# One encoder block on one core: attention fillers dealt anew over the steps, the conv branch's weights released inside the last conv split, and three orderings of the MLP

## The chip, the cores and the metric

The kernel runs on one core of one Trainium2 chip. A core has five engines with their own instruction streams: TensorE (PE in the profile, with its weight loads as PEld), VectorE (DVE), ScalarE (ACT), GpSimd (POOL) and SyncE (SP, which here issues the DMAs). They meet only through semaphores. The metric is the device time of one execution, in microseconds; the median of several executions is given.

## The reference

One layer on an input of 1024 tokens by 1024 channels in float32, with 8 heads of 64, a token grid of 16 by 64 and an MLP of width 4096:

```python
u = rms_norm(x, norm1_g)
q, k, v, cb, cc, ch, ga, gb = split(u @ w_in)
q = rms_norm(q.reshape(B, S, 8, 64), q_norm_g)
k = rms_norm(k.reshape(B, S, 8, 64), k_norm_g)
y_a = neighbourhood_attention(q, k, v, rpb) @ w_attn_branch   # window 8 rows x 16 columns, softmax with a bias
y_b = (cb * conv3(cc * ch, conv_w)) @ w_conv_branch           # depthwise, width 3
merged = sigmoid(ga) * y_a + sigmoid(gb) * y_b
x = x + merged @ w_o
h = rms_norm(x, norm2_g) @ w_mlp_in
x = x + square(relu(h)) @ w_mlp_out
```

## The kernel before

Every float32 matrix product is computed from 16-bit parts: each operand is scaled by a power of two and split into a high and a low half (fp16), and three passes (high by high, high by low, low by high) are summed in PSUM. The high half is a ScalarE copy, the low half a VectorE `scalar_tensor_tensor` (operand times scale minus the high half). The scale needs the sum of squares over a whole weight block: ScalarE squares with a row sum, VectorE adds and casts to a column, and TensorE multiplies that column by ones, one 128x1 matmul that sums over the partitions (`all_sum`, L198 in the profile).

PSUM is handed out as 8 banks in three rings, "d" and "s" of three and "o" of two. The emission order is written out by hand, and each engine runs its own part of that order. `unit` emits the matmuls of a product (L207), then the follow-up work of the product before it (`settle`, the "post"), and then calls `step` and `tick` a given number of times. `step` advances the foreground generators, the follow-ups of finished products; `tick` advances the background ones, which prepare the next weights. A number of ticks per product thus decides where on each engine's stream the background work stands. `apart` makes a generator yield until a given amount of TensorE work has been emitted.

The attention loop runs 64 steps (4 pairs of heads, 8 blocks of 128 tokens, 2 heads), pipelined over 77 turns. In turn k it emits the scores of step k (`at_qk`, L828), the masked maximum on VectorE (`at_max`), the exponential on ScalarE (`at_exp`), the high half of the probabilities (`at_hi`, ScalarE), the low half (`at_lo`, VectorE, `P<-sz,sc,P`), their transposes by DMA from SP's queue for two steps at a time (`at_turn`, L878, PT<-P), and every fourth turn the value products (`at_pv(k - 12)`, L905). Between them stand **fillers**: matmuls of the conv projection (L924, from the generator `conv_mms`), 576 in all. `share(k)` says how many fillers turn k gets, and by that also how much background work `deal(k)` lets in, which uses the estimate that the `Meter` object makes of VectorE's and ScalarE's time. What is left after the loop is emitted at once. In turns 66 to 73 `turn_piece` adds the DMA transposes qD<-gs (L931).

`conv_split` turns a finished conv column into 16-bit halves; the branch weights cB may be scaled only when all four conv columns have their scales (`rowsB`), and `prep` of cB waits for `ch.ready`, which is set behind the loop. After the loop, the first gate (cG, two groups of 24 matmuls), the attention branch (w_wa), the conv branch (w_wb), the other gates and W_o follow.

Both MLP products use a scheme of seven block products in place of eight (`seven`). The first has 16 quads of 7 products of 12 matmuls each (`quad`). A quad's weights are made by `sums1` (GpSimd and ScalarE: sums of blocks, squares) and `prep1` (scale and split, tsum and w in the profile). A quad's posts add the products into `as` on VectorE; then `h_done` applies relu and square on ScalarE and makes four block sums (`sums`, L1278), on GpSimd for q > 1, and writes the result to DRAM. Its arguments wait1 and wait2 hold relu and sums back by so many steps. The activations come from `low(n, part)`, which issues DMA transposes u2T<-v and u2x<-v, one for several forms (L1327). The second MLP product has 28 products whose weights and activations `prep2` makes; the operand with number 16 + n serves its n-th product, in `ORDER`; operands 16 and 17 are made while quads 14 and 15 run.

In the profile of before nearly all VectorE and ScalarE instructions show the line L66, which is the `Meter`'s call; they are told apart by their tiles.

Of the kernel before, what the change touches and what calls it, by code (L numbers as in the profile page):

```python
# [70 lines left out]
def encoder_block(ctx: ExitStack, tc: tile.TileContext, x, weights, cols, gqk, rel, masks, out):  # L71
    nc = tc.nc
    G, T, SP = nc.gpsimd, nc.tensor, nc.sync
    V, A = Meter(nc.vector, 0.96, 150), Meter(nc.scalar, 1.2, 190)

    base = ctx.enter_context(tc.tile_pool(name="base", bufs=1))
    rawp = ctx.enter_context(tc.tile_pool(name="rawp", bufs=5))
# [35 lines left out]
    def tmp(n=1):  # L113
        return cols_of("tmp", n)

    def at(c, i, n=1):
        return slice(c.start + i, c.start + i + n)

    def mul(a, b, out=None):
        out = out or tmp(a.stop - a.start)  # L120
        V.tensor_tensor(sc[:, out], sc[:, a], sc[:, b], op=OP.mult)
        return out
# [13 lines left out]
    fg, bg = [], []  # L136
# [3 lines left out]
    def advance(g):  # L140
        try:
            return next(g) or True
        except StopIteration:
            return False

    def step(n=1):
        for _ in range(n):
            for g in list(fg):
                if not advance(g):
                    fg.remove(g)  # L150

    def tick(n=1):

        for _ in range(n):
            i = 0
            while i < len(bg):
                r = advance(bg[i])
                if not r:
                    bg.pop(i)
                elif r == WAIT and side[0]:  # L160
                    i += 1
                else:
                    break
# [19 lines left out]
    def built(*chs):  # L183

        forced[0] = True
        while not all(ch.split for ch in chs):
            tick()
            step()
        forced[0] = False
# [29 lines left out]
    def settle():  # L219
        while late:  # L220
            late.pop(0)()
# [134 lines left out]
    for (kind, j), pieces in plan():  # L356
        ch = chunks[kind, j] = Chunk(kind, [(nk, sum(n for _, n in cs)) for _, _, nk, cs in pieces],
                                     {"A": "wa", "B": "wb"}.get(kind, "ws"), rows.get(kind, lambda j: g1)(j),
                                     j if kind == "V" else None, 9 if kind in "VQKCGS" else 0)
        ch.first = len(loads)  # L360
        for p, (k, w) in enumerate(ch.widths):
            ch.offs.append(offset)
            if kind != "X" and (kind, j) != ("1", 0) and (kind, j, p) != ("1", 1, 1):
# [3 lines left out]
    cV, cConv, cA, cB, cO, c1, c2, c2x = ([chunks[k, j] for j in range(n)] for k, n in  # L367
                                              (("V", 2), ("C", 4), ("A", 4), ("B", 4), ("O", 2),
                                               ("1", 16), ("2", 4), ("X", 4)))
# [65 lines left out]
    def pow2_half(ss, top, s, inv, more=0):  # L435

        V.tensor_scalar(sci[:, ss], sci[:, ss], EXP, None, op0=OP.bitwise_and)
        yield
        V.tensor_scalar(sci[:, ss], sci[:, ss], 1.0, float(1 << 23), op0=OP.mult, op1=OP.add)
        yield  # L440
        V.tensor_scalar(sci[:, ss], sci[:, ss], 1, EXP, op0=OP.logical_shift_right, op1=OP.bitwise_and)
        yield
        V.tensor_scalar(sci[:, s], sci[:, ss], -1.0, float((190 + top) << 23), op0=OP.mult, op1=OP.add)
        V.tensor_scalar(sci[:, inv], sci[:, ss], 1.0, float((64 - top - more) << 23), op0=OP.mult, op1=OP.add)
        yield
# [131 lines left out]
    for p in range(11):  # L577
# [7 lines left out]
        for q in (p,) if p < 6 else (2 * p - 6, 2 * p - 5):  # L585
            c = q // 2 + 3
# [56 lines left out]
    for n, (kind, b) in enumerate(todo):  # L643
        ch = cQ if kind == "q" else cK
# [103 lines left out]
    def conv_split(j, cv):  # L748
        ch = cConv[j]
        m, s, inv = tmp(), tmp(), tmp()  # L750
        A.activation(BT[:, 1, j].bitcast(BF16), cv, AF.Square, accum_out=sc[:, m])
        yield
        V.tensor_scalar(sc[:, m], sc[:, m], 1e-36, None, op0=OP.max)
        yield
        yield from pow2_half(m, 14, s, inv)
        mul(inv, ch.inv, at(rowsB, j))
        G.tensor_scalar(cv, cv, sc[:, s], 1.0, op0=OP.mult, op1=OP.mult)
        yield
        bh, bl = (BT[:, w, j].rearrange("p (b r c) -> p b r c", b=8, r=16) for w in range(2))
        A.activation(bh, perm(cv), AF.Copy)  # L760
        yield
        pv = perm(cv)
        for b in range(0, 8, 2):
            G.tensor_tensor(bl[:, b:b + 2], pv[:, b:b + 2], bh[:, b:b + 2], op=OP.subtract)
# [175 lines left out]
    def scale_of(am, more, n=3):  # L940

        a, mark = am
        yield from apart(mark, n * 6144, work)
        b, s, inv = cols_of("prep", 1), cols_of("prep", 1), keep()
        yield from all_sum(a, b, anybank(), 1e-36)
        yield from pow2_half(b, 14, s, inv, more)
        return s, inv
# [30 lines left out]
        yield  # L978
        ch.s, ch.inv = yield from scale_of(am, 9, 1)

    meters, debt, mark = (V, A), [0.0, 0.0], [V.ns, A.ns]

    def share(k):
        return 9 if k < 55 else 5 if k < 67 else 2

    def account(k):
        room = 216.0 * share(k) + 570.0
# [13 lines left out]
    for k in range(N + 13):  # L1001
        p, w = k // 16, k % 16
# [37 lines left out]
    emit(1000)  # L1040
    while conv_live or conv_tail or conv_q:
        conv_step(1)
    for ch in cB:
        ch.ready = True
    built(cG)
    p2.close()
    pbias.close()

# [144 lines left out]
    for n in range(8):  # L1193
# [23 lines left out]
        else:  # L1217
# [50 lines left out]
    U2 = (u2T,  # L1268
          w4p.tile([128, 3, 2, 4, 512], F16, name="u2x", bufs=1))
# [53 lines left out]
    def low(n, part):  # L1323

        for a, b, v in pieces(n, part):
            V.tensor_tensor(v[:, :, 1], fv[0][:, a:b], v[:, :, 0], op=OP.subtract)
            SP.dma_start_transpose(U2[a // 4][:, a % 4:a % 4 + b - a, :, :, 128 * n:128 * n + 128]  # L1327
                                   .rearrange("p f s k t -> p (f s k) t"), v.rearrange("p f s k -> p (f s k)"))
        pair_done[0] = n + part

    def form_sums():
# [4 lines left out]
    pe_done, ready = [-2], set()  # L1336
# [32 lines left out]
    def prep1(q):  # L1369

        ch = c1[q]
        s, ch.inv = yield from scale_of(ch.sum, 9, 1)
        yield from gate(q)
        pool, tag = TAGS[q % 3]
        P = P1[q] = pool.tile([128, 7 if q else 8, 2, 512], F16, name="w16_1", tag=tag)
        yield from forms_split(ch, tsum[q], s, P)
        ready.add(q)
        if 1 < q < 15:
            yield from sums1(q + 1)
# [171 lines left out]
    def h_done(q, c0=0, c1=512, wait1=0, wait2=0):  # L1551

        f = AS[q] if c1 < 512 else AS.pop(q)
        v = f[:, :, c0:c1]
        yield from wait(wait1)
        A.activation(v[:, 0:4], v[:, 0:4], AF.Relu)
        yield
        A.activation(v[:, 0:4], v[:, 0:4], AF.Square, scale=sc[:, c1w[q].inv],
                     accum_out=sc[:, at(bsum[q // 4], 4 if c1 < 512 else q % 4)])
        yield  # L1560
        yield from wait(wait2)
        if q > 1:
            yield from sums(v, G)
        else:
            for _ in sums(v, V):
                pass
        if c1 < 512:
            return
        SP.dma_start(HS[q // 4][:, :, q % 4], f)
        live.remove(q)  # L1570
        if q % 4 == 3:
            m = tmp()
            V.tensor_reduce(sc[:, m], sc[:, bsum[q // 4]], axis=AX, op=OP.max)
            yield
            yield from pow2(m, 14, *R[q // 4])
            r_ready[q // 4] = True

    def quad(q, c0=0, c1=512):
        need(q)
        if c0 == 0:  # L1580
            while q - 2 in live:
                step()
            live.add(q)
            AS[q] = w4p.tile([128, 7, 512], F32, name="as", tag="as")
        ps = {}
        z = [AS[q][:, i, c0:c1] for i in range(7)]
        if q == 2:
            z[4:6] = extra

        def post6(ps):  # L1590
            V.tensor_tensor(z[5], ps[6], z[4], op=OP.add)
            if c0:
                post5(ps)

        def post5(ps):
            V.tensor_tensor(z[1], ps[5], z[5], op=OP.subtract)

        def post7(ps):
            V.tensor_tensor(z[6], ps[7], z[5], op=OP.add)
            V.tensor_tensor(z[2], ps[4], z[6], op=OP.add)  # L1600
            V.tensor_tensor(z[3], ps[5], z[6], op=OP.subtract)

        def post3(ps):
            V.tensor_tensor(z[1], ps[3], z[1], op=OP.add)
            if q == 0:
                fg.append(h_done(q, c0, c1, 3, 4 if c0 else 24))
            elif c1 == 512:
                fg.append(h_done(q, 0, c1, *((2, 6) if q == 1 else ())))
        seven(P1[q], actU2, c0, c1, {
            1: lambda ps: A.activation(z[4], ps[1], AF.Copy),  # L1610
            6: post6, 5: None if c0 else post5,
            2: lambda ps: V.tensor_tensor(z[0], ps[2], z[4], op=OP.add),
            7: post7, 3: post3}, 2 if c1 == 512 else 3, 5, (1, 2, 5, 4, 6, 7, 3) if c0 else (1, 6, 5, 4, 2, 7, 3))

    def whole(q):
        quad(q)
# [128 lines left out]
    for n in (2, 3, 4):  # L1745
        h_load(n)
    settle()
    while live:
        step()
    p4.close()  # L1750
# [29 lines left out]
    for n in range(28):  # L1780
        s, o = n // 7, n % 7
# [92 lines left out]
```

## Time and profile before

| | us |
|---|---|
| median of 3 runs | 1238.45 (1238.36 to 1238.69) |
| own time of the profiled execution | 1236.77 |
| its span | 1235.0 |
| TensorE busy | 1196.9 |
| VectorE busy | 936.9 |
| ScalarE busy | 765.9 |
| GpSimd busy | 430.3 |

All instruction times are read on the span, from its start. A timeline row has the start, the length, the engine and line, the operation with its output and inputs, the shapes and the number of instructions drawn together; brackets at the end give the idle time of the engine ahead of it and what ended it. A row of waits has the engine and the line that waited, what it waited for, the total in microseconds, the number of waits and the longest. A row of windows has its stretch, its length, the busy time and the number of instructions of PE, PEld, DVE, ACT and POOL, the granted TensorE clock as a share of the full one, the share of the DMA engines and GB/s. The mean granted clock of the span was 0.994.

### The profile page before, as it was taken

Reading aid. Unit: us, or ns where it says so; the run is one execution under the profiler, and the core shown is the slowest. Engines: PE = TensorE matmul, PEld = TensorE weight load, DVE = VectorE, ACT = ScalarE, POOL = GpSimd, SP = SyncE. Lnnn points to the kernel's source line nnn. Section 1 sums busy time; section 2 is a strip of 40 time slices with the busy share of each in tenths; the row PEclk is TensorE's granted clock in tenths of the full one; section 3 lists DMA queues with packets and bytes.
Section 4 is the critical chain, followed back from the end, with each engine's and each line's share of the span. In section 5 each row is a group of like instructions: output and inputs, shape, how many; then the busy total and the mean of one; then the engine's idle time right before and its main releaser. Section 6 shows DMA issues by size and latency. Waiting matters only on the chain.

```text
span 1235.0 us, 16691 instructions
## 1 busy us (share of the span) xinstructions
PE 1196.9 (97%) x6102; PEld 576.9 (47%) x6102; DVE 936.9 (76%) x1747; ACT 765.9 (62%) x1185; POOL 430.3 (35%) x289
## 2 busy tenths in 40 slices
PE   5989999999899999999999999999999999999998
PEld 3534445555444444444458444444444444444444
DVE  6668778888558786877878664555547999999997
ACT  6777667768644454535768777777775763646430
POOL 2440003232212111101003466655648373463562
PEclk8999999999899999999999999999999999999999
DMA  6558455565761211216096653454474844435202
GB/s 258 107 200 178 103 118 112 116 153 105 131 154 34 69 52 51 69 35 255 18 174 152 205 170 137 162 187 142 140 290 162 313 155 159 168 116 222 103 35 103
DMA packets 170867, 173.34 MB, mean 140 GB/s; under 512 B 131488, under 2 KB 132000, under 8 KB 166688
## 3 DMA queue, kind: packets, MB, share of 16 engines
q1 hardware_dynamic: 170784, 172.27, 47.2%
q8 instruction: 48, 0.79, 0.3%
q14 instruction: 35, 0.29, 0.1%
HBM read 102.51 MB, written 37.75 MB: 114 GB/s over the span
## 4 chain that ended last, share of the span: by engine, by line
PE 40%; DVE 6%; ACT 2%; issue 2%; DMA 1%; DVEq 0%; ACTq 0%
PE ps_d L207 16%; PE ps_s L207 14%; PE ps_o L207 10%; DVE as L66 1%; DVE ops L66 1%; DVE w L66 1%; DVE form L66 1%; ACT as L66 1%; DVE v L66 1%; DMA u2T<-v 1%; DMA u2x<-v 1%; ACT ops L66 1%; DVE x L66 0%; DVE sc L66 0%; ACT u2x L66 0%
## 5 line engine op out<-in xcount | busy, mean ns | idle before, releaser
L207 PEld LDWEIGHTS <-ops 128*128 128x128 f16 x1356 | 132.4, 98 | 159.9 <-issue 2.7
L207 PEld LDWEIGHTS <-w 128*128 128x128 f16 x1368 | 132.8, 98 | 143.5 <-issue 3.8
L924 PE MATMUL ps_d<-uT,w_ws 128*128 128x512 f16 x576 | 136.7, 382 | 0.0
L207 PE MATMUL ps_s<-ops 128*128 128x512 f16 (+1 forms) x528 | 118.3, 374 | 0.0
L207 PE MATMUL ps_d<-ops 128*128 128x512 f16 x504 | 115.6, 379 | 0.0
L66 ACT ACTIVATE ops<-hf,sc 128x2048 f16<-128x2048 f32 x26 | 52.0, 1999 | 94.0 <-PE ps_d L207 52.7
L207 PE MATMUL ps_d<-u2T,w 128*128 128x512 f16 (+1 forms) x504 | 110.3, 371 | 0.0
L1074 POOL TENSOR_TENSOR tsum<-raw 128x512 f32<-128x512 f32 x28 | 46.6, 1677 | 148.1 <-ACT raw L66 148.1
L207 PEld LDWEIGHTS <-uT 128*128 128x128 f16 x648 | 64.9, 101 | 70.5 <-issue 5.6
L1278 POOL TENSOR_TENSOR as<-as 128x512 f32<-128x512 f32 x56 | 76.7, 1370 | 41.4 <-ACT as L66 38.1
L207 PEld LDWEIGHTS <-w_s 128*128 128x128 f16 x588 | 56.9, 98 | 68.6 <-DVE w_s L66 0.6
L924 PEld LDWEIGHTS <-w_ws 128*128 128x128 f16 x576 | 56.1, 98 | 59.7 <-issue 2.0
L207 PE MATMUL ps_s<-u2x,w 128*128 128x512 f16 (+1 forms) x348 | 78.6, 375 | 0.0
L207 PE MATMUL ps_o<-ops 128*128 128x512 f16 x324 | 74.3, 379 | 2.4 <-DVE as L66 2.4
L66 DVE SCALAR_TENSOR_TENSOR ops<-hf,sc,ops 128x2048 f16<-128x2048 f32 x26 | 71.7, 2759 | 5.7 <-ACT ops L66 5.7
L66 ACT ACTIVATE raw<-raw,sc 128x256 f32<-128x256 f32 x172 | 71.1, 494 | 6.7 <-DMA raw<-in_weights 6.7
L66 DVE TENSOR_TENSOR as<-ps_s,as 128x512 f32<-128x512 f32 (+1 forms) x38 | 23.4, 616 | 58.5 <-ACT as L66 57.9
L66 DVE TENSOR_SCALAR sc<-sc 128x1 int32<-128x1 int32 (+3 forms) x380 | 57.6, 167 | 12.9 <-ACT sq L66 4.3
L1074 POOL TENSOR_TENSOR gsum<-raw 128x512 f32<-128x512 f32 x14 | 18.5, 1340 | 136.8 <-issue 52.3
L66 ACT ACTIVATE w<-raw,sc 128x512 f16<-128x512 f32 (+1 forms) x29 | 25.4, 920 | 50.8 <-DVE sc L66 50.8
L66 ACT ACTIVATE sz<-sz,sc 128x384 f32<-128x384 f32 (+1 forms) x64 | 37.2, 581 | 26.8 <-DVE sc L66 26.6
L66 DVE SCALAR_TENSOR_TENSOR w_ws<-raw,sc,w_ws 128x512 f16<-128x512 f32 (+2 forms) x72 | 48.5, 712 | 6.7 <-ACT w_ws L66 6.7
(261 smaller groups left out, 2548.6 us busy)
## 6 DMA issues: line engine op xcount, KB each, us to landing
raw<-in_weights SPq DMA_DIRECT2D x89, 512.0 KB, 5.5
hs<-as SPq DMA_DIRECT2D x16, 1792.0 KB, 8.7
hf<-hs SPq DMA_DIRECT2D x26, 1024.0 KB, 6.7
w2x<-in_weights SPq DMA_DIRECT2D x16, 512.0 KB, 8.3
raw<-in_weights SPq DMA_DIRECT2D x16, 384.0 KB, 3.7
xt<-in_x SPq DMA_DIRECT2D x8, 512.0 KB, 9.8
gs<-s SPq DMA_DIRECT2D x4, 1024.0 KB, 6.4
x<-in_x SPq DMA_DIRECT2D x8, 512.0 KB, 10.0
```

The source lines that it names most:

```text
L66: return f(out, *a, **kw)
L207: T.matmul(ps, l, r, start=a, stop=b)
L924: T.matmul(ps, l, r, start=a, stop=b)
L1074: G.tensor_tensor(t[:, o], a, b, op=OP.add)
L1278: sub.tensor_tensor(z[o], z[a], z[b], op=op)
```

## The change

- The filler table `share` is another: 9 a turn for the first six turns, then 8 up to turn 54, then 6, 7 and 4, in place of 9 up to turn 54, 5 and 2. The limit of `deal` and `account` follows it.
- `V` and `A` are the plain engines, and the `Meter` exists only for the attention loop.
- cB is set ready inside `conv_split(3, ...)`, when `rowsB` is complete.
- For the last pair of token blocks (n == 3) `low` issues one DMA transpose for each form, in place of one for four and one for three.
- In `prep1` the ones matmul of quads 3 to 7 stands two products behind the sum, in place of one.
- `h_done`: quad 14's block sums run on VectorE; quads 2 to 5 hold relu back by three steps, quad 14 holds the sums back by two.
- Quad 15 has three ticks a product in place of five, and behind it the program ticks until operand 17 has been emitted before it steps the live quads to their end.

```diff
-    V, A = Meter(nc.vector, 0.96, 150), Meter(nc.scalar, 1.2, 190)
+    V, A = nc.vector, nc.scalar
...
         yield from pow2_half(m, 14, s, inv)
         mul(inv, ch.inv, at(rowsB, j))
+        if j == 3:
+            for c in cB:
+                c.ready = True
...
-    meters, debt, mark = (V, A), [0.0, 0.0], [V.ns, A.ns]
+    meters = V, A = Meter(nc.vector, 0.96, 150), Meter(nc.scalar, 1.2, 190)
+    debt, mark = [0.0, 0.0], [0.0, 0.0]
 
     def share(k):
-        return 9 if k < 55 else 5 if k < 67 else 2
+        return 9 if k < 6 else 8 if k < 55 else 6 if k < 64 else 7 if k < 73 else 4
...
-    for ch in cB:
-        ch.ready = True
     built(cG)
+    V, A = nc.vector, nc.scalar
...
             V.tensor_tensor(v[:, :, 1], fv[0][:, a:b], v[:, :, 0], op=OP.subtract)
-            SP.dma_start_transpose(U2[a // 4][:, a % 4:a % 4 + b - a, :, :, 128 * n:128 * n + 128]
-                                   .rearrange("p f s k t -> p (f s k) t"), v.rearrange("p f s k -> p (f s k)"))
+            for c, d in [(f, f + 1) for f in range(a, b)] if n == 3 else [(a, b)]:
+                SP.dma_start_transpose(U2[c // 4][:, c % 4:c % 4 + d - c, :, :, 128 * n:128 * n + 128]
+                                       .rearrange("p f s k t -> p (f s k) t"),
+                                       v[:, c - a:d - a].rearrange("p f s k -> p (f s k)"))
...
-        s, ch.inv = yield from scale_of(ch.sum, 9, 1)
+        s, ch.inv = yield from scale_of(ch.sum, 9, 2 if 2 < q < 8 else 1)
...
-        if q > 1:
+        if q > 1 and q != 14:
             yield from sums(v, G)
...
-                fg.append(h_done(q, 0, c1, *((2, 6) if q == 1 else ())))
+                fg.append(h_done(q, 0, c1, *((2, 6) if q == 1 else (3, 0) if q < 6 else (0, 2) if q == 14 else ())))
...
-            7: post7, 3: post3}, 2 if c1 == 512 else 3, 5, (1, 2, 5, 4, 6, 7, 3) if c0 else (1, 6, 5, 4, 2, 7, 3))
+            7: post7, 3: post3}, 2 if c1 == 512 else 3, 5 if q < 15 else 3, (1, 2, 5, 4, 6, 7, 3) if c0 else (1, 6, 5, 4, 2, 7, 3))
...
     settle()
+    while 17 not in ready:
+        tick()
     while live:
         step()
```

## The prediction

> **What bounds the kernel now.** I read first the page's head, busy times and chain, then TensorE's waits, then the timelines at the places where it waits.
>
> ```profile
> span 1235.0 us, 16691 instructions
> PE 1196.9 (97%) x6102; PEld 576.9 (47%) x6102; DVE 936.9 (76%) x1747; ACT 765.9 (62%) x1185; POOL 430.3 (35%) x289
> PE 40%; DVE 6%; ACT 2%; issue 2%; DMA 1%; DVEq 0%; ACTq 0%
> ...
> PE ps_o L905 <- DMA PT<-P: 5.8, 3, 3.0
> PE ps_o L207 <- DVE as L66: 4.8, 2, 2.4
> PE ps_d L207 <- ACT w_wb L66: 1.5, 1, 1.5
> PE ps_s L198 <- DVE ones L66: 0.8, 1, 0.8
> PE ps_s L207 <- DMA u2T<-v: 0.2, 1, 0.2
> ```
>
> TensorE is busy 97% of the span and no matmul is taken away, so all there is to win lies in its waits (total, count, longest) and in stretches at half clock. The change touches three regions: the end of the attention loop (5.8), the conv branch weight (1.5) and the MLP's first half (0.8, 0.2, and 4.8 in two waits, one inside that half and one at the passage to the second product).
>
> The end of the attention, on TensorE (start, length, idle ahead in brackets) and by windows (length, then busy PE, PEld, DVE, ACT, POOL, granted clock, DMA share, GB/s):
>
> ```profile
> 318.53 1.18 PE L905 MATMUL ps_o<-PT,vT 128*64 128x256 f16 x24 [0.36 <-DMA PT<-P]
> 319.64 3.19 PE L924 MATMUL ps_d<-uT,w_ws 128*128 128x512 f16 x14
> 325.79 2.13 PE L905 MATMUL ps_o<-PT,vT 128*64 128x256 f16 x24 [2.96 <-DMA PT<-P]
> 327.86 2.53 PE L924 MATMUL ps_d<-uT,w_ws 128*128 128x512 f16 x8
> 332.88 1.81 PE L905 MATMUL ps_o<-PT,vT 128*64 128x256 f16 x18 [2.49 <-DMA PT<-P]
> 337.26 1.02 PE L207 MATMUL ps_o<-uT,w_ws 128*128 128x512 f16 x4
> ...
> 166.00:326.70 160.70, 157.17 (x998) 79.95 (x998) 134.24 (x401) 119.72 (x285) 36.02 (x50) 1.00 0.58 122
> 325.75:329.16 3.41, 3.37 (x28) 2.15 (x29) 0.96 (x3) 3.38 (x8) 1.73 (x3) 0.50 1.27 156
> 332.58:335.99 3.41, 3.11 (x22) 1.90 (x23) 0.63 (x1) 0.60 (x1) 1.07 (x1) 0.50 0.50 113
> ```
>
> The value products (L905) wait for probabilities, because the fillers (L924) are used up: 14, then 8, are left between the last three. Behind both long waits stands a stretch of 3.41 us at clock 0.50; it costs half of its busy time, (3.37 + 3.11) / 2 = 3.2.
>
> **Attention: the new share of fillers.** The matmuls are the same. Counted in the instruction order of the changed program, 31 fillers stand between the value products that had 20, then 28 for 14, 28 for 8, and 13 for 9 after the last. Upper bound of the gain: 5.8 of waits and 3.2 of half clock, 9.0; the cG products would start at 337.26 - 9.0 = 328.3. Whether that is reached hangs on the softmax chain of the last step, not on TensorE:
>
> ```profile
> 326.24 0.47 DVE L66 SCALAR_TENSOR_TENSOR P<-sz,sc,P 128x256 f16<-128x256 f32 x1
> 326.23 3.38 SPq L931 DMA_TRANSPOSE qD<-gs  x2
> 329.66 1.31 SPq L878 DMA_TRANSPOSE PT<-P  x1
> ...
> DVE sc L66 <- ACT sz L66: 7.5, 7, 1.6
> DVE z L66 <- PE ps_d L924: 6.5, 4, 2.7
> DVE w_ws L66 <- ACT w_ws L66: 4.3, 7, 0.9
> DVE sz L66 <- DMA kD<-k: 3.0, 1, 3.0
> ```
>
> The last low half ends at 326.71, its transpose goes out behind two others on SP's queue, and the product starts at 332.88, 6.2 later. Those two transposes keep their place, so the 6.2 stays; with the value product at full clock (18/24 of 1.18, 0.9) and 13 fillers at 3.19/14 (3.0), the loop ends 10.1 after that low half. VectorE is the second engine of this stretch: it was busy 134.24 of the 160.7 us from 166 to 326.7, waited 11.8 for ScalarE, 3.0 for a DMA, and 6.5 for TensorE. With one filler fewer per step (3.19/14 = 0.23 us) the steps come faster, and VectorE can follow only as far as its waits for TensorE go: 6.5. So the low half lands between 320.2 (all of it gone) and 326.7 (none). I take 320.2: waits will come anew, but eight of VectorE's operations also move behind this low half in the changed order (699 stand ahead of it, 707 before), some 1.5 us. The end is then 330.3, **gain 7.0**. If VectorE gives only half (323.3) the end is 333.4, gain 3.9. That is this edit's likely range, 4 to 9.0, and no gain at all is a rival below. What would be late next is VectorE itself.
>
> The Meter object is only made later; it emits the same instructions, cost 0.
>
> **cB ready one group earlier.** The 1.5 us wait is for the high half of w_wb, whose scale is computed after a sum by TensorE that stands behind the branch's first products:
>
> ```profile
> 354.49 2.85 PE L207 MATMUL ps_d<-bT,w_wb 128*128 128x512 f16 x12 [1.52 <-ACT w_wb L66]
> 353.93 1.71 ACT L66 ACTIVATE w_wb<-raw,sc 128x256 f16<-128x256 f32 x4 [5.42 <-DVE sc L66]
> ```
>
> In the changed program that one-column matmul stands between the two cG groups, 24 + 24 matmuls ahead of where it stood, some 11 us at 0.23. ScalarE had been idle 5.42 us before w_wb, so it can move up. **Gain 1.5**, bounds 0 and 1.5; the gate's sigmoid is queued ahead of it on ScalarE but has its products first.
>
> **MLP, first half.** The 2.4 us wait at 706.45:
>
> ```profile
> 697.10 2.96 DVE L66 SCALAR_TENSOR_TENSOR w<-raw,sc,w 128x512 f16<-128x512 f32 x2
> 699.98 4.49 DVE L66 SCALAR_TENSOR_TENSOR w<-tsum,sc,w 128x1024 f16<-128x1024 f32 x2
> 705.71 1.28 DVE L66 TENSOR_TENSOR as<-ps_o,as 128x512 f32<-128x512 f32 x2
> 706.45 2.75 PE L207 MATMUL ps_o<-u2T,w 128*128 128x512 f16 x12 [2.41 <-DVE as L66]
> 718.14 2.47 DVE L66 SCALAR_TENSOR_TENSOR w<-tsum,sc,w 128x1024 f16<-128x1024 f32 x2
> 701.47 4.13 POOL L1074 TENSOR_TENSOR tsum<-tsum,raw 128x512 f32<-128x512 f32 x2 [0.28 <-ACT tsum L66]
> ```
>
> Four weight splits (7.4 us) stand on VectorE ahead of the additions that empty the PSUM bank. With the scale one product later (q = 3 to 7) and the sums held back, the additions precede the splits in the changed order. The next weights are then one product later, against the seven of a quad that cover them. Gain 2.4, and 0.8 for the wait on the ones column shortly behind it; the split transposes take at most the 0.2. **Sum 3.4**, bounds 0 and 3.4. The five more issues on SP carry the same data; priced at the smallest transpose above, 7 x 1.31 = 9.2 us in place of one pair, and were they not overlapped the last form would be some 0.5 us late, which I keep as the lower end.
>
> The split of the same size took 4.49 beside GpSimd's sums and 2.47 without. The Trainium skill ("SBUF — State Buffer", Who interferes with whom) says that a VectorE instruction with two SBUF inputs contends with a GpSimd instruction that reads SBUF; these rows agree, and by it the four sums moved to VectorE below are themselves open to such a slowdown.
>
> **The passage to the second product: the loss.** Three edits meet: three ticks a product in quad 15 instead of five, quad 14's four sums on VectorE, and the loop that holds the program until operand 17 is ready. In the changed order the first one-column sum of the second product's weights stands behind five products of quad 15 instead of one, and the low halves of operand 16 come on VectorE after quad 15's last addition. Rows for the sum:
>
> ```profile
> 921.68 1.91 ACT L66 ACTIVATE as<-as 128x2048 f32<-128x2048 f32 x1 [3.53 <-DVE as L66]
> 923.62 2.00 ACT L66 ACTIVATE as<-as,sc 128x2048 f32<-128x2048 f32 x1
> 912.66 1.15 ACT L66 ACTIVATE ops<-raw,sc 128x1024 bf16<-128x1024 f32 x1
> 694.32 2.86 DVE L66 TENSOR_TENSOR as<-as 128x512 f32<-128x512 f32 x4
> 928.12 2.44 DVE L66 SCALAR_TENSOR_TENSOR ops<-h,sc,ops 128x2048 f16<-128x2048 f32 x1 [1.03 <-ACT ops L66]
> 935.61 2.75 PE L207 MATMUL ps_s<-u2x,w 128*128 128x512 f16 x12
> 938.20 2.75 PE L207 MATMUL ps_o<-ops 128*128 128x512 f16 x12
> 948.51 2.75 PE L207 MATMUL ps_o<-ops 128*128 128x512 f16 x12 [2.38 <-DVE as L66]
> ```
>
> Let t be the start of quad 15. Last addition of quad 14, t + 0.9; then on ScalarE relu 1.9, a raw square 1.2, the square of the quad 2.0, two squares of w2x of the same width, 2 x 2.0 and some 0.1 of issue each: t + 10.2. On VectorE sum and cast 0.7, an addition 0.7, the four sums 2.9: t + 14.5; then five additions at 0.64 and some small scale work at about 0.2 each, 4.2: t + 18.7; the last addition 0.7, the low half of h 2.4, the first raw low half 1.2 (half of 2.47): t + 23.0, and t + 25 if GpSimd slows the low halves as above (4.49 for 2.47). TensorE is through quad 15 at t + 7 x 2.59 = 18.1 (products of 12 matmuls follow each other at 938.20 - 935.61). So it **waits 4.9 to 6.9**, I take 5.2, in place of the 2.38 that went before: loss 2.8. A wait of this length also falls mostly into one 3.41 us window, and the waits of 2.96 and 2.49 above were each followed by half clock while 2.41 and 2.38 were not: 1.5 more (half of 3.1). **Loss 4.3**, bounds 0 (the work has moved up far enough) and 6.2 (6.9 - 2.4 + 1.7).
>
> The Trainium skill ("TensorE: Matmul & The Clock Gate", Part 1: The HAM clock gate) puts the half clock behind at least one idle window of about 3.4 us; the waits of 2.96 and 2.49 here were shorter and had it, so the trace differs. By the rule the 1.5 would fall away unless the wait covers a whole window, and the sum would be 1.5 better.
>
> **Sum:** -7.0 - 1.5 - 3.4 + 4.3 = -7.6 on the profiled execution's own 1236.8 (span 1235.0 and 1.8 around it). The median of the runs shown, 1238.45, is 1.7 above that; I subtract from it: **1230.8**.
>
> **Rivals.** (a) VectorE holds the attention. Its low half stays at 326.7, only the two half-clock stretches shrink a little (0.5). For it: 134 of 161 us busy, and 14.8 of its waits not TensorE's. Against: the 6.5 that are. -0.5 - 1.5 - 3.4 + 4.3 = -1.1: 1237.3. (b) Slower: the passage costs far more. Operand 16, then 17 and 18, are made in one line on VectorE; if each one's low halves run at 4.49 instead of 2.47 beside GpSimd's sums, the first wait is 6.9, each of the next two 2 to 3 more, with three half-clock stretches at 1.7: 6.9 + 5 + 5.1 - 2.4 = 14.6. With the attention's low gain of 4.0: -4.0 - 1.5 - 3.4 + 14.6 = +5.7: 1244. It decides from a loss of 8.9 there on. For it: no slack was found for operand 17, which by my sums is ready as it is needed. Against: GpSimd has lost quad 14's sums, which were its long work there. (c) No loss at the passage: -11.9, 1226.5. For it: the products may start on the high halves. Against: their low halves follow soon. (d) The fillers do nothing: the share only moves the same waits to earlier steps, where the steps go at VectorE's pace; with the MLP's gain and loss cancelling, 1238 as before.
>
> **How the numbers follow.** Forecast 0.55, (a) 0.13, (b) 0.12, (c) 0.12, (d) 0.08. The likeliest case's own range: gains of 4 + 1.5 + 2.4 less 4.3 up to 9.0 + 4.9 less 2.8, 1227 to 1235. The range takes in (c), (a) and (d) at 1225 and 1239, leaving out (b) and the tails. A change of 0.2%, 2.5 us, is what can be told from none. Faster: the forecast, (c) and a part of (a), 0.72; same: the rest of (a) and (d), 0.15; slower: (b), 0.13.
>
> **What would show it.** In the profile of the changed kernel: the waits at the value products' line under 1.5 us in all, no 0.50 window there, cG's first products near 330; low half of the last step near 320 (326 would be rival (a)). No wait on w_wb, none of 2.4 on `as` in the MLP's first half. One wait of about 5 us on `ops` after quad 15, followed by one window at 0.50; several such waits would be (b). The forecast is wrong if either of the two large terms, 7.0 and 4.3, is off by more than 4.

## The result, and the profile after

The changed kernel took 1257.42 us (median of four runs, 1255.56 to 1258.03) against 1238.4 for the kernel before on the same chip: a ratio of 1.0155, 95% interval 1.0137 to 1.0173. It is 19 us slower, where 7.6 less had been forecast. The profiled execution took 1255.56 us, its span 1253.8. The page's head, busy times and chain:

```profile
span 1253.8 us, 16695 instructions
PE 1202.1 (96%) x6102; PEld 576.3 (46%) x6102; DVE 966.8 (77%) x1751; ACT 766.0 (61%) x1185; POOL 427.7 (34%) x285
PE 35%; DVE 6%; ACT 6%; DMA 4%; issue 1%; POOL 1%; SPq 0%; DVEq 0%; ACTq 0%; POOLq 0%
```

ScalarE and GpSimd have no more work than before. VectorE is busy 30 us longer, with only four instructions more; run e6 below shows where. In the chain, ScalarE went from 2% to 6% and DMA from 1% to 4%: what has grown most is waits. TensorE's waits from 650 us on, the MLP (line numbers are now those of the changed file, and only the attention still shows L66):

```profile
PE ps_d L207 <- DVE w L1090: 7.3, 2, 3.9
PE ps_o L207 <- ACT ops L1708: 7.1, 1, 7.1
PE ps_d L198 <- DVE sc L129: 5.5, 1, 5.5
PE ps_o L207 <- DVE ops L1712: 2.2, 1, 2.2
PE ps_s L198 <- DVE ones L940: 1.0, 1, 1.0
PE ps_o L198 <- DVE ones L940: 1.0, 1, 1.0
PE ps_o L207 <- DVE w L1090: 0.7, 1, 0.7
```

Behind them stand half-clock stretches (length, busy PE, PEld, DVE, ACT, POOL, clock, DMA, GB/s):

```profile
733.46:740.29 6.83, 4.54 (x12) 1.65 (x12) 3.81 (x15) 1.82 (x4) 5.66 (x5) 0.50 0.00 0
760.77:767.60 6.83, 5.87 (x15) 2.12 (x16) 4.80 (x9) 1.48 (x4) 5.75 (x4) 0.50 0.01 2
951.91:962.15 10.24, 4.70 (x11) 1.53 (x11) 10.17 (x12) 4.08 (x3) 4.09 (x2) 0.50 1.02 326
```

The end of the attention came out nearly as worked out. TensorE and VectorE there:

```profile
318.15 1.67 PE L927 MATMUL ps_d<-uT,w_ws 128*128 128x512 f16 x7 [2.04 <-DVE cv L66]
319.75 1.18 PE L908 MATMUL ps_o<-PT,vT 128*64 128x256 f16 x24
327.20 1.01 PE L908 MATMUL ps_o<-PT,vT 128*64 128x256 f16 x18
330.96 5.34 PE L207 MATMUL ps_o<-uT,w_ws 128*128 128x512 f16 x24
...
319.77 0.47 DVE L66 SCALAR_TENSOR_TENSOR P<-sz,sc,P 128x256 f16<-128x256 f32 x1
```

The last low half starts at 319.77 (before 326.24), the last two value products wait for nothing and run at full clock, and the cG products start at 330.96 in place of 337.26.

The account, in spans: attention -6.3; the 1.5 us at w_wb gone; in the MLP's first half 15.5 us of waits (5.5 + 7.3 + 1.0 + 1.0 + 0.7) and (4.54 + 5.87) / 2 = 5.2 of half clock, against 3.9 of waits before (the 3.4 of the forecast and 0.5 ahead of its first sum, where one of the 1.0 now stands), +16.8; at the passage 7.1 + 2.2 of waits and 4.70 / 2 of half clock against 2.4, +9.3. That is +18.3 of the 18.8 by which the span grew.

Where the MLP's first half loses is seen on ScalarE and SP's queue:

```profile
699.28 0.60 ACT L1615 ACTIVATE as<-ps_d 128x512 f32<-128x512 f32 x1 [2.69 <-DMA hs<-as]
...
701.37 1.90 ACT L1561 ACTIVATE as<-as 128x2048 f32<-128x2048 f32 x1
...
706.99 1.99 ACT L1563 ACTIVATE as<-as,sc 128x2048 f32<-128x2048 f32 x1
...
715.15 0.53 SPq L1574 DMA_DIRECT2D hs<-as  x1
...
721.80 0.60 ACT L1615 ACTIVATE as<-ps_d 128x512 f32<-128x512 f32 x1 [12.72 <-DMA hs<-as]
...
727.82 1.99 ACT L1563 ACTIVATE as<-as,sc 128x2048 f32<-128x2048 f32 x1
...
742.01 0.53 SPq L1574 DMA_DIRECT2D hs<-as  x1
...
748.62 0.60 ACT L1615 ACTIVATE as<-ps_o 128x512 f32<-128x512 f32 x1 [13.30 <-PE ps_s L207]
```

L1615 is the first copy of a quad into its `as` buffer, of which there are two. The copy at 721.80 waits 12.72 us for the DMA that empties the buffer of two quads earlier, issued at 715.15. Everything that ScalarE has behind it waits too: the high halves of the next weights, and so TensorE. From copy to copy it takes 22.5 and 26.8 us, where the products of a quad take 18.1. (The releaser of the third copy is named as TensorE; the DMA issued at 742.01 had landed 0.1 us before it.)

### The profile page after: what moved, and what is told of

It reads as the page before. It is cut to its first block, busy times and chain, and to the rows that moved or that the text cites. A ratio compares the mean times of both kernels' runs of the same rounds, so it can differ in the third digit from the quotient of the medians.

```text
span 1253.8 us, 16695 instructions
## 1 busy us (share of the span) xinstructions
PE 1202.1 (96%) x6102; PEld 576.3 (46%) x6102; DVE 966.8 (77%) x1751; ACT 766.0 (61%) x1185; POOL 427.7 (34%) x285
## 4 chain that ended last, share of the span: by engine, by line
PE 35%; DVE 6%; ACT 6%; DMA 4%; issue 1%; POOL 1%; SPq 0%; DVEq 0%; ACTq 0%; POOLq 0%
PE ps_d L207 13%; PE ps_s L207 12%; PE ps_o L207 9%; DMA hs<-as 2%; DVE w L1090 1%; ACT raw L959 1%; DVE as L1281 1%; DMA w2x<-in_weights 1%; ACT tsum L968 1%; ACT as L1561 1%; ACT as L1563 1%; ACT w L1094 1%; DVE form L1281 1%; DMA u2x<-v 1%; POOL as L1281 1%
## 5 line engine op out<-in xcount | busy, mean ns | idle before, releaser
L207 PE MATMUL ps_d<-u2x,w 128*128 128x512 f16 (+1 forms) x324 | 73.0, 375 | 7.3 <-DVE w L1090 7.3
L959 ACT ACTIVATE raw<-raw,sc 128x256 f32<-128x256 f32 x164 | 67.7, 494 | 11.9 <-DMA raw<-in_weights 11.8
L207 PE MATMUL ps_o<-u2T,w 128*128 128x512 f16 (+1 forms) x324 | 72.7, 374 | 0.8 <-DVE w L1090 0.7
L1090 DVE SCALAR_TENSOR_TENSOR w<-raw,sc,w 128x512 f16<-128x512 f32 (+1 forms) x28 | 45.3, 1645 | 21.5 <-ACT w L1094 20.9
L66 ACT ACTIVATE sz<-sz,sc 128x384 f32<-128x384 f32 (+1 forms) x64 | 37.2, 581 | 23.6 <-DVE sc L66 23.4
L207 PE MATMUL ps_d<-u2T,w 128*128 128x512 f16 (+1 forms) x240 | 51.2, 363 | 0.0
L207 PE MATMUL ps_s<-u2x,w 128*128 128x512 f16 (+1 forms) x216 | 50.5, 385 | 0.0
L1717 POOL TENSOR_TENSOR raw<-raw 128x1024 f32<-128x1024 f32 x8 | 30.7, 3861 | 45.1 <-DVE ops L1712 45.1
```

What stands on the lines that cost most here:

```text
L66: return f(out, *a, **kw)
L207: T.matmul(ps, l, r, start=a, stop=b)
L959: A.activation(v, v, AF.Copy, scale=sc[:, at(g, 4 * i + k)])
L1090: V.scalar_tensor_tensor(o(1), w, sc[:, s], o(0), op0=OP.mult, op1=OP.subtract)
L1717: G.tensor_tensor(w11[i2], w11[i2], w12[i2], op=OP.add)
```

## The experiments

By "lag" I mean the ones matmul of quads 3 to 7 one product later, by "hold" the pair (3, 0) for relu of quads 2 to 5, by "passage" the three edits at quads 14 and 15. Ratios are to the kernel before on the same chip, whose median was 1238.2 to 1240.3; where runs of different chips are compared, it is by ratio.

| run | what it has of the MLP's edits | us | ratio, 95% |
|---|---|---|---|
| the change | lag, hold, passage, split transposes | 1257.42 | 1.0155 (1.0137 to 1.0173) |
| e1 | all but hold | 1235.51 | 0.9976 (0.9966 to 0.9985) |
| e2 | all but passage | 1258.81 | 1.0164 (1.0148 to 1.0180) |
| e3 | lag, split | 1237.75 | 0.9993 (0.9982 to 1.0004) |
| e4 | none | 1232.12 | 0.9946 (0.9931 to 0.9961) |
| e5 | split | 1232.47 | 0.9931 (0.9915 to 0.9948) |
| e6 | lag | 1239.83 | 0.9997 (0.9988 to 1.0007) |
| e7 | hold | 1234.00 | 0.9950 (0.9935 to 0.9965) |
| e8 | passage | 1227.79 | 0.9896 (0.9881 to 0.9911) |
| e9 | all but lag | 1227.92 | 0.9905 (0.9890 to 0.9919) |
| e10 | passage, split | 1227.69 | 0.9903 (0.9890 to 0.9916) |
| e11 | e10 with lag at quad 3 alone | 1277.66 | 1.0304 (1.0290 to 1.0319) |
| e12 | e1 with five ticks | 1234.01 | 0.9951 (0.9938 to 0.9965) |
| e13 | e10 with five ticks | 1229.37 | 0.9922 (0.9907 to 0.9938) |
| e14 | e10, quad 14's sums on GpSimd | 1227.68 | 0.9912 (0.9896 to 0.9928) |
| e15 | e10 without the loop for operand 17 | 1228.55 | 0.9915 (0.9898 to 0.9933) |

All sixteen have the new filler share and cB early.

### The four first: hold, passage, both, neither

e1 takes the hold out, e2 the passage, e3 both. The edits of e1, then of e2:

```diff
-                fg.append(h_done(q, 0, c1, *((2, 6) if q == 1 else (3, 0) if q < 6 else (0, 2) if q == 14 else ())))
+                fg.append(h_done(q, 0, c1, *((2, 6) if q == 1 else (0, 2) if q == 14 else ())))
```

```diff
-        if q > 1 and q != 14:
+        if q > 1:
...
-                fg.append(h_done(q, 0, c1, *((2, 6) if q == 1 else (3, 0) if q < 6 else (0, 2) if q == 14 else ())))
+                fg.append(h_done(q, 0, c1, *((2, 6) if q == 1 else (3, 0) if q < 6 else ())))
...
-            7: post7, 3: post3}, 2 if c1 == 512 else 3, 5 if q < 15 else 3, (1, 2, 5, 4, 6, 7, 3) if c0 else (1, 6, 5, 4, 2, 7, 3))
+            7: post7, 3: post3}, 2 if c1 == 512 else 3, 5, (1, 2, 5, 4, 6, 7, 3) if c0 else (1, 6, 5, 4, 2, 7, 3))
...
-    while 17 not in ready:
-        tick()
```

e4 is e3 with these two undone as well:

```diff
-        s, ch.inv = yield from scale_of(ch.sum, 9, 2 if 2 < q < 8 else 1)
+        s, ch.inv = yield from scale_of(ch.sum, 9, 1)
...
-            for c, d in [(f, f + 1) for f in range(a, b)] if n == 3 else [(a, b)]:
+            for c, d in [(a, b)]:
```

> The changed kernel, but quads 2 to 5 no longer hold relu back (the pair (3, 0) taken out); all else as changed. Theory A, the two `as` buffers: held back by three steps, relu of quad q stands on ScalarE behind the first copy of quad q + 1, which itself waits for the DMA that empties quad q - 1's buffer (2.7, 12.7 and 11.0 us at the copy in the changed kernel), so the quads 2 to 5 run in a serial loop of some 25 us in place of 18. Then the waits of 5.55, 0.69, 3.86, 3.45 and 1.03 in the MLP's first half are gone together with their half-clock windows (two of 6.8 us, some 6 us lost): some 20 us off, 1237 (1234 to 1241), and no copy waits for hs<-as. Theory B, the ones matmul one product later (scale lag) and the split of weights behind it: the waits on w stay, time above 1250.

> The changed kernel, but the passage to the second product is the old one: five ticks in quad 15, quad 14's sums on GpSimd without hold, no loop until operand 17. Theory A: the waits of 7.1 and 2.2 us and the half-clock stretch behind them give way to the 2.4 of before: 11 us off, 1246.5 (1244 to 1249), while the waits in the first half stay. Theory B, the passage is only late because the quads before it were late (hs and the w2x loads land late): less than 4 us off, above 1253.

> Both undone: no hold of relu in quads 2 to 5, the old passage. If the two causes are independent and all: 1257.4 - 20 - 11 = 1226.5 (1225 to 1231). If either only moved a wait to another place, above 1235.

> The kernel before with the new filler share, the Meter change and cB ready early alone; the whole MLP as before. Theory A: the gain of 7.1 us that stands at the start of the MLP in the two traces (first ones matmul there 653.3 against 660.4) is kept to the end: 1231.3 (1229 to 1233). Theory B: it is given back in the MLP, whose DMAs then start earlier against each other: 1235 or more. Compared with e3 it prices the scale lag and the split transposes: e3 lower by up to 3.4 if they do what was forecast.

e1 came out as theory A had it: 22 us off, and every wait of TensorE in the first half gone; of its waits from 650 to 1000 us only the 7.1 and the 2.2 at the passage are left. (One copy still waits 4.3 us for its buffer, where none was expected.) e2 did not: with the old passage the time stayed where it was. So the passage loses in the changed kernel, but not by its own three edits. e3 says the same: with hold and passage undone there was no gain against before, though the attention's 6 us were in it. e4 has these and stands 0.0054 below before, 6.7 us. So something between e3 and e4, the lag or the split transposes, costs e3 about 6 us, and these showed as waits at the passage in e3. TensorE's waits of e3 from 690 us on:

```profile
PE ps_d L207 <- DVE ops L1712: 4.4, 1, 4.4
PE ps_o L207 <- DVE ops L1712: 3.7, 2, 3.2
PE ps_d L198 <- DVE ones L940: 2.2, 1, 2.2
```

In the first half there is none: there the lag does what I had forecast.

### Each of the MLP's edits alone

Each of these is e4 with one edit of the change put back.

> e4 (new share and cB, old MLP at 1232.1) with one more edit alone: a DMA transpose for each form at the last pair. Theory: the wait of 0.24 on u2T goes or stays, 1231.9 (1231 to 1233). Rival: five more issues on SP push the weight loads back and cost a microsecond or more, 1233.5 and above.

> e4 with the ones matmul of quads 3 to 7 one product later alone. Theory: each of the first such quads moves the background work back by a product and it never comes back (in e3 the ones matmuls stand some two products later than in e4 right up to quad 15), so the MLP's first half loses its waits of 2.4 and 0.8 but the passage gets waits of 2.2, 3.2, 0.5 and 4.4 and half-clock windows as in e3: 1237.7 (1236 to 1239). Rival: the split transposes made e3 slower, the lag alone helps: 1229 to 1231.

> e4 with the hold of relu in quads 2 to 5 alone, no lag. Theory A (two `as` buffers): the copies of the quads after wait for hs<-as by 10 us or more each whether or not the scale lags; with e1's difference of 22 it comes to 1250 (1246 to 1256). Rival: the hold only hurts together with the lag, below 1240.

> e4 with the new passage alone (three ticks in quad 15, quad 14's sums on VectorE with a hold of two, the loop until operand 17). My forecast for this part, made without lag: 4.3 us lost, 1236.4 (1234 to 1240), with one wait of about 5 us ahead of operand 16's product. Rival: quad 14's sums on VectorE run beside GpSimd's sums of w2x and take 7 us in place of 2.9 as in the changed kernel, so the loss is 8 to 11: 1240 to 1243.

The split transposes neither gain nor lose (e5 and e4 overlap). The lag alone costs 0.0051, 6.3 us, as its theory had it, again as waits at the passage. TensorE's waits of e6 from 690 to 975 us, where e4 has 2.4 and 0.8 in the first half and 2.4 at the passage:

```profile
PE ps_d L207 <- DVE ops L1712: 5.6, 1, 5.6
PE ps_o L207 <- DVE ops L1712: 4.6, 4, 1.8
PE ps_d L198 <- DVE ones L940: 1.7, 1, 1.7
```

The lag has a second effect. VectorE is busy 965.0 us in e6 against 937.3 in e4, and most of the difference lies in the weight splits: the 28 of tsum take 45.8 us in place of 36.7, the 14 of raw of the same size 27.8 in place of 18.9. In the period that was read they run beside GpSimd's sums with the lag (e6: splits from 847.51 to 854.1, sums from 843.95 to 849.61 and from 851.44 on); without it GpSimd stands idle meanwhile (e10: splits from 802.05 to 806.4, GpSimd idle from 800.2 to 805.4). What this adds to the 6.3 was not measured apart.

The hold alone costs nothing that can be told: here theory A, that two buffers and the hold are all of it, fell. The passage alone gains 0.0050, 6 us, on the side of neither of the two expectations, which both had a loss. Why the hold is cheap without the lag is read from ScalarE. First its waits for the `as` buffer in e7 from 690 to 800 us, then a quad of e9, which has the hold but no lag:

```profile
ACT as L1615 <- DMA hs<-as: 17.2, 4, 5.0
```

```profile
717.78 0.60 ACT L1615 ACTIVATE as<-ps_d 128x512 f32<-128x512 f32 x1 [1.45 <-POOL tsum L1077]
718.27 1.90 ACT L1561 ACTIVATE as<-as 128x2048 f32<-128x2048 f32 x1
720.21 2.00 ACT L1563 ACTIVATE as<-as,sc 128x2048 f32<-128x2048 f32 x1
...
736.38 0.60 ACT L1615 ACTIVATE as<-ps_d 128x512 f32<-128x512 f32 x1 [1.90 <-DMA hs<-as]
```

The copies wait for the buffer here as well, but the square follows relu at once, and the loop from copy to copy is 18.6 us, hardly more than the 18.1 of the products. With the lag, the splits and squares of the next weights stand between relu and square (701.37 to 706.99, 722.90 to 727.82 above) or GpSimd has the next weights' sums among the quad's four: in the loop that starts at 748.62 relu and square follow at once, but the four sums stretch from 753.2 to 766.6, where they take 5.3 us in e9. The loop becomes 22 to 27. No run gave `as` a third buffer, which would have tried the loop directly.

### The lag undone, the best version, and a smaller lag

e9 is the change with the first edit below alone, e10 has that and the edit of e1, e11 is e10 with the second edit, and e12 is e1 with five ticks a product in quad 15, as in e2.

```diff
-        s, ch.inv = yield from scale_of(ch.sum, 9, 2 if 2 < q < 8 else 1)
+        s, ch.inv = yield from scale_of(ch.sum, 9, 1)
```

```diff
-        s, ch.inv = yield from scale_of(ch.sum, 9, 1)
+        s, ch.inv = yield from scale_of(ch.sum, 9, 2 if q == 3 else 1)
```

> The changed kernel with one edit undone: the ones matmul of quads 3 to 7 again one product behind its sum. Everything else as changed, the hold of relu too. Theory C, the lag is the one culprit, by itself 6 to 7 us (e6 against e4) and the lever by which the hold closes into a loop of 25 us per quad (e7: the hold without lag has copy waits of 3.5 to 5.0 but costs 2): 1257.4 falls to e8 plus the 2 of the hold, 1230 (1227 to 1233). Theory A, the hold by itself: above 1250.

> The changed kernel without lag and without hold: new share, cB early, split transposes, new passage. Theory C: e8 (1227.8) and the split transposes, which took the 0.79 and 0.24 waits away in e5 without a gain that could be told: 1227.3 (1226 to 1229). Left on TensorE should be 2.06 at the end of the attention and 2.4 in the MLP's first half.

> e10 with the lag at quad 3 alone, where the wait of 2.4 stands. Theory C (each lag moves all later background work back by one product for good): the 2.4 goes, and with only one product lost the passage stays without a wait: 1225 (1223.5 to 1227). Rival: one product is already too much, a wait of 2 to 5 us comes at the passage and the time is 1228 to 1232.

> e1 (lag, no hold, new passage: 1235.5, waits of 7.09 and 2.23 ahead of operand 16) with five ticks a product in quad 15 in place of three. Theory: under the lag the background work is three products late and three ticks cannot catch it up, so with five the ones matmul of the second product's weights stands after the first product of quad 15 again, quad 14's sums take 2.9 in place of 7.1 and the 7.09 goes: 1229 (1227 to 1232). Rival: the order of quad 14's sums on VectorE is what holds it, no change, 1234 to 1237.

e9 settles the main question: one number, 2 in place of 1, is worth 0.0250, 31 us, in the changed kernel. Without it the change is faster than before by 0.0095 (0.0081 to 0.0110). e10, without the hold too, is the same within its interval; either beats both kernels. Its waits from 650 us on:

```profile
PE ps_o L207 <- DVE as L1606: 2.4, 1, 2.4
PE ps_o L198 <- DVE ones L940: 1.1, 1, 1.1
PE ps_d L198 <- DVE ones L940: 0.2, 1, 0.2
```

The 2.4 is the old wait of the first half, which the lag was to remove. e11 tried to remove it with the lag at one quad, and was the slowest of all: 50 us above e10, outside both of its expectations. Its waits:

```profile
PE ps_d L198 <- DVE ones L940: 27.7, 8, 5.3
PE ps_d L198 <- DVE sc L127: 10.0, 3, 3.8
PE ps_o L198 <- DVE ones L940: 0.9, 1, 0.9
PE ps_o L207 <- DVE as L1606: 0.6, 1, 0.6
```

Eleven waits of 2.9 to 5.3 us, one in each quad. So a lag at one quad does move all the later background work, but the new place is a bad one. One period of it:

```profile
812.49 1.91 ACT L1561 ACTIVATE as<-as 128x2048 f32<-128x2048 f32 x1 [6.17 <-DVE as L1609]
814.30 1.69 ACT L959 ACTIVATE raw<-raw,sc 128x256 f32<-128x256 f32 x4
815.90 1.99 ACT L1563 ACTIVATE as<-as,sc 128x2048 f32<-128x2048 f32 x1
817.88 1.69 ACT L959 ACTIVATE raw<-raw,sc 128x256 f32<-128x256 f32 x4
...
820.64 1.06 ACT L968 ACTIVATE tsum<-raw 128x1024 f32<-128x1024 f32 x1
...
823.95 0.16 DVE L940 CAST ones<-sc 128x1 bf16<-128x1 f32 x1
824.16 0.16 PE L198 MATMUL ps_d<-ones 128*128 128x1 bf16 x1 [3.07 <-DVE sc L127]
```

ScalarE's scaling and squares of the next weights are queued behind relu, which can start only when the quad's last addition is done (6.17 us idle); the ones matmul stands a fixed number of products behind, and the column is cast 0.2 us before TensorE takes it. Eight of the eleven are followed by a half-clock stretch. In e10 the same scaling is ahead of relu, and TensorE takes the column later than it is cast.

In e12, five ticks brought the wait for operand 16 from 7.1 to 2.6, but one of 1.6 came ahead of the ones matmul, and quad 14's sums still took 6.4 us. By the ratio it gained 0.0025 on e1; the 1227 to 1232 that I expected is missed. Under the lag, more ticks in quad 15 mend the passage only in part.

### The passage, edit by edit

Each undoes one part of e2's edit in e10: e13 the ticks (five again), e14 quad 14's sums on VectorE and their hold, e15 the loop.

> e10 (1227.7: no lag, no hold) with five ticks a product in quad 15 again. Theory D: the three ticks place quad 15's additions ahead of operand 17's low halves on VectorE, which was the wait of 2.4 on `as` before; with five the wait comes back, 1230 (1229 to 1231). Rival, the ticks do nothing and quad 14's sums on VectorE are the gain: 1227.7 as e10.

> e10 with quad 14's four sums on GpSimd again and without their hold. Theory D: GpSimd's 8.1 us beside VectorE's splits slows the low halves (4.5 for 2.5), 1229 (1228 to 1231). Rival: as e10, 1227.7, as the three ticks alone clear the passage.

> e10 without the loop until operand 17. Theory: quad 15's relu and square then come on ScalarE ahead of operand 17's high halves, some 4 us later for operand 17; its product has slack of a few microseconds, so 1227.7 to 1230. Rival: much worse, above 1232, the loop is what makes three ticks bearable.

With five ticks the wait on quad 15's additions is there again, and with three it is not. TensorE's waits of e13 from 900 to 975 us:

```profile
PE ps_o L207 <- DVE as L1606: 1.8, 1, 1.8
```

Its time is 0.0019 above e10; the intervals overlap, so it is the trace more than the measured time that says it: the three ticks, which I had priced as the loss, are what clears the passage when there is no lag. e14 and e15 show no wait at the passage and no difference that can be told; what quad 14's sums and the loop are worth stays open.

The traces show less for the passage than the times. From the first to the second one-column sum of the second product's weights it is 75.08 us in e4 and 72.54 in e8, a gain of 2.5, which is the wait. In its trace e8 is ahead of e4 by 4.2 us already at the first one-column sum after 650 us (651.64 against 655.81), before any edit in which the two differ; so about 2.5 of the 6 us is shown to be the passage's, and the rest is not located.

## Why the prediction was wrong, point by point

- **Attention**: right. The end of the last low half was put at 320.2 and came at 320.24; the end of the loop at 330.3 came at 330.96. The gain of 7.0 was 6.3. The missing 0.7 is TensorE's own: the last value product started 7.0 behind the low half in place of 6.2 and waited for nothing, since TensorE had lost 2.04 us just before at a new wait for VectorE (`cv`), which the sum had left out. (The case in which VectorE gives half was worked out 0.15 too low: half of 6.5 puts the low half at 323.45, the gain at 3.7.) Rivals (a) and (d) fell. e4, with the attention and cB alone, has 6.7 of the forecast 8.5.
- **cB**: right; no wait on w_wb is left.
- **Split transposes**: right, nothing (e5).
- **The MLP's first half, "gain 3.4"**: the step that failed. I said that the additions would then precede the splits, which they did, and that "the next weights are then one product later, against the seven of a quad that cover them". That counted the delay once and priced it at nothing. Each quad's preparation starts the next one's, so the delays of quads 3 to 7 add up and move all the background work behind them: counted in the traces, the six ones matmuls from 650 us on stand 13, 8, 8, 8 and 8 products apart with the lag (e1) and 11, 8, 7, 7 and 7 without (e10), five products more, and then 7 apart in both up to the passage. Measured for the lag alone (e6): the 2.4 and the 0.8 are gone there, and 6.3 is lost in all; with the hold 22 more (the change against e1). The price does not follow the number of products: e11, with one delay, lost 50. What decides is what the moved work meets in the queues of ScalarE and VectorE, and for that the forecast had no term.
- **The hold of relu** I costed at nothing, in half a sentence that speaks of the sums held back, and left out what is queued behind the copy on ScalarE. Two buffers, and relu behind the next quad's copy, close a loop of copy, relu, square, sums, DMA, copy. Its price depends on what the lag puts in the loop: nothing told alone (e7), 22 us with the lag.
- **The passage, "loss 4.3"**: the place and kind of the loss were right in the changed kernel, a wait of 7.1 for operand 16 where 5.2 had been taken, and 9.3 in all. The cause was not. The order that I read, five products of quad 15 ahead of the ones matmul, I ascribed to the three ticks. It came mostly from the lag: with the three ticks and no lag it is one product (e10), with the lag and five ticks four (e6). By themselves the three edits gain 3.5 to 6 us (e10 against e5, e8 against e4). Rival (b), which begins at a loss of 8.9 here, was nearest in size, but by luck: its reason was operands 17 and 18, and no rival had a loss in the first half, where most of it came.

So the whole change is some 12 us of gain without lag and hold (e10) and 31 of loss with them, the 19 that were measured.

The size of the miss in the changed kernel's passage has one more row. The 7.1 is ended by operand 16's high half on ScalarE, and the 2.2 behind it by its low half; that low half came 28.2 us after the start of quad 15 (929.80), where the sum had 23.0. Quad 14's four sums on VectorE beside GpSimd's sums of the second product's weights, and the ones matmul just ahead of them:

```profile
942.75 0.17 PE L198 MATMUL ps_s<-ones 128*128 128x1 bf16 x1
...
942.84 7.09 DVE L1281 TENSOR_TENSOR as<-as 128x512 f32<-128x512 f32 x4
943.10 2.80 POOL L1677 TENSOR_TENSOR h<-raw,w2x 128x1024 f32<-128x1024 f32 x1
```

In e8, where GpSimd is done with those sums by then, the same four took 2.86:

```profile
917.66 2.86 DVE L1281 TENSOR_TENSOR as<-as 128x512 f32<-128x512 f32 x4
```

The difference, 4.2 us, is on the path, as the scale of operand 16 stands behind the four sums on VectorE; the forecast, which had 2.9 for them, should have taken it into its sum. That is the slowdown that the rule of the Trainium skill quoted with the forecast ("SBUF — State Buffer", Who interferes with whom) speaks of; the two rows agree with it. Another 1.6 us is a wait of ScalarE, ahead of its last square, for the load of w2x.

## What to carry to other kernels

In a schedule written by hand, a delay put into a chain in which each link starts the next moves every later stage: ask what the moved work meets there, down to where the chain ends, and not only what the stage gains that gets the slack. Before holding work back on an engine, ask which buffer it frees and whether the work that waits for that buffer is queued ahead of it on the same engine; if so there is a loop, and its length against the stage's own is the price. And two edits that were each measured harmless or mild (0 and 6 us here, each alone) may cost far more together, so the pair has to be run: 31 us here, the change against e10.

## What the hardware showed that was not expected

The half clock follows the share of TensorE's busy time in stretches of 3.41 us on a grid of their own, not the length of a wait. The same wait of 2.4 us, in two kernels and on that grid:

```profile
697.48:700.89 3.41, 1.21 (x6) 0.46 (x5) 3.38 (x4) 0.00 (x0) 2.69 (x2) 1.00 1.01 273
700.89:704.30 3.41, 3.19 (x8) 1.13 (x8) 0.76 (x2) 2.58 (x2) 0.00 (x0) 0.50 0.66 262
```

```profile
701.21:704.63 3.42, 2.82 (x14) 1.18 (x12) 3.42 (x3) 0.12 (x2) 3.08 (x2) 1.00 1.02 255
704.63:708.04 3.41, 1.59 (x8) 0.76 (x8) 2.33 (x4) 1.02 (x1) 0.97 (x1) 1.00 1.02 392
```

In e10 (first) the wait fell into one stretch, which was busy 1.21 of 3.41 us, and the next one ran at 0.50, for 1.6 us. In the kernel before (second) it lay across two, busy 2.82 and 1.59, and the clock stayed at 1.00. In e4, a stretch that was busy 1.36 us (315.40 to 318.81) was followed by half clock. So from full clock the limit lies between 1.36 and 1.59 busy us of 3.41, in the stretches above. All seventeen traces, from 20 to 1200 us and cut on their own grids, agree: each of 55 full-clock stretches that half clock followed was busy 1.39 us or less, and of the 5737 that full clock followed one was busy 1.39 and all others 1.46 or more. From half clock it takes more to get out: a stretch that was busy 2.45 us (760.77 to 764.18 in the changed kernel) was followed by another at 0.50. The Trainium skill ("TensorE: Matmul & The Clock Gate", Part 1: The HAM clock gate) gives the free-running window of 3413 ns, which the trace bears out, and at least one idle window as the condition; here windows with a third of their time busy were enough. Two executions of one kernel may so differ by some 1.6 us (an estimate from the e10 rows) for nothing but where a wait of 2.4 us falls.
